# Attention: high and low parts of the probabilities joined in one product, meta keys in one product last in its unit, two output banks, dense products spread evenly over the units

## The chip, the cores and the metric

The kernel runs on one core of one Trainium2 chip. The metric is the device time of one execution in microseconds (us); of several runs the median is taken. The engines are named as in the profile: PE (TensorE, the matrix products; PEld is its loading of weights), DVE (VectorE), ACT (ScalarE), POOL (GpSimd) and SP (SyncE, which here only issues DMAs).

## The reference, cut to what matters

A block of a streaming encoder on 1024 tokens of width 1024, with 16 meta tokens ahead of them. The change lies in the attention with forgetting (8 heads of 64 channels) and in the gates that are computed beside it:

```python
h = concatenate([meta, x])                     # 16 + 1024 tokens
xn = rmsnorm(h, norm_mix_g)
q, k, v, f_logit, u, gates = split(xn @ w_in)
cum_f = cumsum(log_sigmoid(f_logit + b_forget))
s = q.k / sqrt(64) + cum_f[t] - cum_f[s]       # for s <= t, else -1e30
y_a = (softmax(s) @ v) @ w_attn_out
y_s = glu(gelu(s5(u)) @ w_glu)                 # state-space branch
g = sigmoid(gates)                             # two sets of 1024 channels
h = h + (g[:1024] * y_a + g[1024:] * y_s) @ w_o
h = h + conv_ffn(rmsnorm(h, norm_ffn_g))
out = rmsnorm(h, norm_final_g)[16:]            # meta tokens dropped
```

All is float32.

## The kernel before

**Stages.** One program goes through norm, projections, state-space branch, GLU, values, attention, output projection and ConvFFN in turn, with the next stage's loads running ahead. To keep float32 precision, each operand is split into a high part in the faster format fp32r and the rest as a low part; a dense product is three products (high by high, low by high, high by low: lines 170 to 172, `dense_steps`).

**Values.** The tile `vt` holds, for each tile of 128 keys and each head, 128 columns: 64 channels of the values' high part and 64 of the low part. The 16 meta keys are key tile 0, in rows 0 to 15.

**Attention.** The heads are taken in four pairs (loop `pr`). A pair has ten units: for each of its two heads one small unit (the 16 meta tokens as queries) and four big units of 256 queries (two tiles of 128). `scores()` makes a unit's probabilities: blocks of up to 512 columns, each in two products (lines 817 and 818, into the banks `sp`), a maximum on DVE (line 823), then the exponential on ACT and the scaling on POOL. `pv()` multiplies them by the values. The scores of a unit are issued ahead of `pv()` of the unit before, so PE has other work while the softmax runs.

**`pv()`.** The probabilities have queries in rows; for the product they are turned, so that keys lie in rows. The keys are taken in groups: the meta keys first, by themselves, then two tiles of 128 at a time, so that a big unit has one group of meta keys and one to four others. For a group, `turn()` transposes each 128x128 block on PE into the bank `tp` (line 860), ACT copies this to the high part `th` (line 867), and DVE subtracts it from the bank and writes the low part `tl` (line 868, shown as L137, the line of the helper `split_lo`). Then each key tile takes one product with `th` (line 881) and one with `tl` (line 882), both into the one output bank `po`, whose rows 0 to 63 gather what comes from the values' high part, rows 64 to 127 the rest. `turn()` of the next group is issued ahead of the products of this one. Where a key tile lies after the first query tile, half of its block is not transposed; POOL sets that half of `th` and `tl` to zero. At the end ACT copies the lower rows of `po` to `ot` (line 885) and DVE adds the halves into `ob` (line 886). The next unit's first product must wait until this has been read.

**The dense products in between.** A generator (`stream`) yields the dense products of the next pair's q and k projection and of chunks of the gates; `fill()` takes some of them at each group of a big unit. There are 28 such places a pair, and each takes what is left over the places left, rounded up. The pairs have 288, 216, 216 and 216 of these products (the first takes 24 of its own ahead). A dependency without a semaphore keeps each lot behind the fifth last group's product (`marks`, `SLACK`). Apart from it, the order in which PE takes instructions is set by the tile scheduler from the program's order and its own estimate of times. Accumulating dense products have three banks `mm`.

## Time and profile before

| | before |
|---|---|
| median of 3 runs | 1444.85 us (1443.14 to 1447.14) |
| profiled execution | 1444.9 us |
| its span | 1443.1 us |
| granted TensorE clock, mean | 0.998 |
| PE busy in the span | 1422.4 us (99%) |
| DVE, ACT, POOL busy | 1073.0, 722.2, 762.9 us |
| attention stage (first dense product after the values, to the last of its dense products) | about 340.6 to 622.3 us |

A row of PE in order of time has the start and duration in us, the engine, the line in the kernel, the operation with the tile written and the tiles read, the part of PE's array that it takes (rows*columns), its size (columns streamed after the x), and how many such instructions in a row it stands for. The duration is that from entering the array to leaving it, so that following products overlap; the distance from start to start says what one costs.

### The profile page before, as it was taken

To read this page: it belongs to the slowest core of one execution; us is meant where nothing else is said; L and a number is where in the kernel's file an instruction comes from. 1 tells how busy PE (TensorE), PEld (TensorE's weight loads), DVE (VectorE), ACT (ScalarE), POOL (GpSimd) and SP (SyncE) were. 2 spreads that over 40 slices of the span, in tenths; PEclk is the share of its full clock that TensorE was granted. 3 is DMA by queue.
4 is the path that set the end of the run, shared out by engine and by line. 5 is a ranking of instruction groups with operands and counts; after the bars stand their busy time and mean duration, and the time that the engine had idled before them with its cause. 6 is when DMAs were issued, how large, how long until landed. Compare 5 with 4: busy or idle time off the path is not lost.

```text
span 1443.1 us, 26612 instructions
## 1 busy us (share of the span) xinstructions
PE 1422.4 (99%) x9655; PEld 1346.8 (93%) x9655; DVE 1073.0 (74%) x2203; ACT 722.2 (50%) x1419; POOL 762.9 (53%) x887
## 2 busy tenths in 40 slices
PE   8999999999999999999999999999999999999997
PEld 8999999988999999999879999999999999888886
DVE  7999788843657676656469987788877876788857
ACT  7646585423656565533646544444434445644433
POOL 1542248632456556515871335555555545888794
PEclk9999999999999999999999999999999999999999
DMA  8676644530147422167964156667753327864433
GB/s 303 169 182 164 153 102 151 150 106 30 38 130 165 126 66 67 45 222 244 267 147 142 63 139 170 171 164 190 187 136 116 92 71 262 328 204 142 123 87 117
DMA packets 92968, 214.06 MB, mean 148 GB/s; under 512 B 15090, under 2 KB 22898, under 8 KB 92452
## 3 DMA queue, kind: packets, MB, share of 16 engines
q1 hardware_dynamic: 73124, 166.32, 35.2%
q0 software_dynamic: 17696, 41.29, 15.2%
q10 hardware_dynamic: 2016, 4.74, 0.9%
q8 instruction: 76, 1.25, 0.4%
q14 instruction: 56, 0.46, 0.1%
HBM read 170.88 MB, written 71.71 MB: 168 GB/s over the span
## 4 chain that ended last, share of the span: by engine, by line
PE 91%; DVE 5%; DMA 1%; ACT 1%; issue 1%; POOL 0%; SPq 0%; POOLq 0%; ACTq 0%; DVEq 0%
PE mm L172 5%; PE mm L170 5%; PE mm L171 5%; PE sp L232 4%; PE sp L233 4%; PE sp L234 4%; PE tp L232 3%; PE tp L233 3%; PE tp L234 3%; PE mm L232 3%; PE mm L234 3%; PE mm L233 3%; PE tp L860 3%; PE mm L1557 2%; PE mm L1555 2%; PE mm L1556 2%
## 5 line engine op out<-in xcount | busy, mean ns | idle before, releaser
L170 PE MATMUL mm<-xhi,whi 128*128 128x342 f32 (+2 forms) x480 | 156.8, 327 | 1.0 <-DVE q L137 1.0
L172 PE MATMUL mm<-xhi,wlo 128*128 128x342 f32 (+2 forms) x480 | 155.3, 324 | 0.0
L171 PE MATMUL mm<-xlo,whi 128*128 128x342 f32 (+2 forms) x480 | 155.2, 324 | 0.0
L1183 POOL TENSOR_TENSOR ov<-ov,og 128x1024 f32<-128x1024 f32 x21 | 50.8, 2421 | 117.1 <-ACT og L1182 114.7
L137 DVE TENSOR_TENSOR sw<-sf,sw 128x512 fp32r<-128x512 f32 x72 | 73.5, 1021 | 45.6 <-ACT sw L1174 45.3
L1174 ACT CAST sw<-sf 128x512 fp32r<-128x512 f32 x72 | 44.9, 623 | 111.3 <-POOL sf L1321 82.3
L170 PEld LDWEIGHTS mm<-xhi,whi 128*128 128x128 f32 x480 | 90.5, 188 | 2.1 <-PE sp L818 0.8
L172 PEld LDWEIGHTS mm<-xhi,wlo 128*128 128x128 f32 x480 | 90.2, 188 | 0.6 <-issue 0.2
L171 PEld LDWEIGHTS mm<-xlo,whi 128*128 128x128 f32 x480 | 90.4, 188 | 0.2
L867 ACT CAST th<-tp 128x256 fp32r<-128x256 f32 (+3 forms) x120 | 56.1, 471 | 62.5 <-PE tp L860 30.2
L137 DVE TENSOR_TENSOR tl<-tp,th 128x256 fp32r<-128x256 f32 (+3 forms) x120 | 65.2, 547 | 25.9 <-ACT th L867 24.5
L1321 POOL TENSOR_TENSOR sf<-raw,sf 128x512 f32<-128x512 f32 x36 | 63.5, 1764 | 38.7 <-DVE sw L137 38.6
L1321 POOL TENSOR_TENSOR sf<-raw 128x512 f32<-128x512 f32 x36 | 49.1, 1364 | 62.2 <-ACT sw L1174 22.2
L234 PE MATMUL mm<-xhi,sw 128*128 128x258 f32 (+1 forms) x288 | 81.0, 281 | 0.0
L232 PE MATMUL mm<-xhi,sw 128*128 128x258 f32 (+1 forms) x288 | 80.8, 281 | 0.0
L233 PE MATMUL mm<-xlo,sw 128*128 128x258 f32 (+1 forms) x288 | 80.7, 280 | 0.0
L832 POOL TENSOR_SCALAR pt<-pt,nm 128x144 f32<-128x144 f32 (+4 forms) x72 | 52.1, 736 | 49.9 <-DVE nm L831 48.9
L1373 DVE SCALAR_TENSOR_TENSOR ov<-hv,cwt,ov 128x1024 f32<-128x1024 f32 x36 | 68.5, 1904 | 0.4 <-ACT ov L1371 0.4
L1174 ACT CAST sw<-raw 128x512 fp32r<-128x512 f32 x70 | 43.0, 620 | 46.6 <-PE sp L234 22.6
L830 ACT ACTIVATE pt<-pt,nm 128x144 f32<-128x144 f32 (+4 forms) x72 | 52.9, 735 | 25.7 <-DVE nm L829 25.2
L137 DVE TENSOR_TENSOR sw<-raw,sw 128x512 fp32r<-128x512 f32 x70 | 58.3, 837 | 5.3 <-ACT sw L1174 5.1
L823 DVE CUSTOM_DVE_ANT_0 pt<-sp,fb 128x328 f32<-128x328 f32 (+8 forms) x112 | 46.4, 430 | 21.2 <-PE sp L818 12.6
(722 smaller groups left out, 5720.7 us busy)
## 6 DMA issues: line engine op xcount, KB each, us to landing
raw<-in_w_up_dram SPq DMA_DIRECT2D x44, 512.0 KB, 3.8
t_d<-in_w_dn_dram POOLq DMA_DIRECT2D x44, 256.0 KB, 6.7
wr<-t_d SPq DMA_DIRECT2D x44, 256.0 KB, 3.8
ar<-a_d SPq DMA_DIRECT2D x41, 256.0 KB, 5.2
a_d<-ov SPq DMA_DIRECT2D x18, 512.0 KB, 2.6
wr<-in_w_dn_dram SPq DMA_DIRECT2D x33, 256.0 KB, 4.0
t_d<-in_w_dn_dram SPq DMA_DIRECT2D x22, 256.0 KB, 4.7
t_d<-t_d SPq DMA_DIRECT2D x22, 256.0 KB, 4.6
```

Of the source, the lines that this page charges most:

```text
L137: return eng.tensor_tensor(out_, src, hi.bitcast(F), ALU.subtract)
L170: yield PE.matmul(ps, whi[:, i, :], ahi[:, i], start=(i == 0), stop=False)
L171: yield PE.matmul(ps, whi[:, i, :], alo[:, i], start=False, stop=False)
L172: yield PE.matmul(ps, wlo[:, i, :], ahi[:, i], start=False, stop=(i == k - 1))
L232: PE.matmul(ps, a[0][:, i], bh, start=(i == 0 and not joins), stop=False, skip_group_check=True)
L233: PE.matmul(ps, a[0][:, i], bl, start=False, stop=False, skip_group_check=True)
L234: PE.matmul(ps, a[1][:, i], bh, start=False, stop=(i == kh - 1), skip_group_check=True)
L830: S.activation(pt[:n, :kc], pt[:n, :kc], AF.Exp, bias=nm[:n, 1:2], scale=0.125, accum_out=nm[:n, 2:3])
L867: S.copy(th[:kn, z:tw], tp[:kn, z:tw])
L1174: S.copy(hi, src)
L1321: sums.append(GP.tensor_tensor(f_, a, b, op))
L1373: V.scalar_tensor_tensor(out=o, in0=h_[:, j:SEQ + j], scalar=cwc(j, m), in1=o, op0=ALU.mult, op1=ALU.add)
```

## The change

1. *Joined products.* `th` and `tl` become the two halves of one tile `tt`, and the two products of a key tile one product of 512 columns: both read the same weights, and the bank's 512 columns hold the high parts' result in the first half and the low parts' in the second. Where a key tile lies after the first query tile, only the second query tile's columns of both halves are streamed (2x128), so nothing is set to zero any more.
2. *Meta keys.* The meta values are stored twice, in rows 0 to 15 and 32 to 47 of `vt`. The meta keys' probabilities are turned into rows 0 to 15 (16 columns of weights a transpose, where 128 were taken before), the high part goes to rows 0 to 15 of a tile `tm` that is otherwise zero, the low part to rows 32 to 47, and one product of 256 columns (16 in a small unit) gives both. It is the last of its unit.
3. *Output.* The output bank is by turns `po` and one of the dense products' three `mm`. ACT copies the lower rows straight into `ob`, DVE adds the upper rows, and in a big unit the second half of the bank in a further addition.
4. *Spread.* `fill()` takes a share per unit: each big unit 1, divided evenly over its groups and one place more ahead of them; a small unit 0.4; 8.8 units a pair. In the first pair a chunk of the gates comes ahead of the q and k projection.
5. *Gates in this stage* are scaled (POOL) and stored (SP) in thirds as they come, except the last chunk.

```diff
@@ -489,14 +489,20 @@
 
     def gate_chunk(i, pl, tanh):
         whi, wlo = gate0[1:] if i == KD else wchunk(w_g[i], KD, GP, act=not tanh)
-        if tanh:
+        whole = tanh and pl is not gp_ and i == KD - 1
+        if whole:
             gs = pl.tile([P, LQ], F, tag="gs", name="gs", bufs=1)
         for t, n in QBLK[::-1] if i == KD else QBLK:
             ps = mm_ps()
             yield from dense_steps(ps[:, :n], whi, wlo, xhi[:, :, T0 + t:T0 + t + n],
                                    xlo[:, :, T0 + t:T0 + t + n], KD)
-            if tanh:
+            if whole:
                 S.activation(gs[:, t:t + n], ps[:, :n], AF.Tanh, scale=0.5)
+            elif tanh:
+                gs = pl.tile([P, LQ // 3], F, tag="gs", name="gs", bufs=2)
+                S.activation(gs, ps[:, :n], AF.Tanh, scale=0.5)
+                GP.tensor_scalar(gs, gs, 0.5, 0.5, ALU.mult, ALU.add)
+                SY.dma_start(g_d[P * i:P * i + P, t:t + n], gs)
             else:
                 if i == KD:
                     gs = g0s[:, t:t + n]
@@ -504,12 +510,9 @@
                     gs = pl.tile([P, LQ // 3], F, tag="gs", name="gs", bufs=2)
                 S.activation(gs, ps[:, :n], AF.Sigmoid)
                 GP.dma_start(g_d[P * i:P * i + P, t:t + n], gs)
-        if tanh:
+        if whole:
             GP.tensor_scalar(gs, gs, 0.5, 0.5, ALU.mult, ALU.add)
-            if pl is not gp_ and i == KD - 1:
-                okeep["g"] = gs
-            else:
-                SY.dma_start(g_d[P * i:P * i + P], gs)
+            okeep["g"] = gs
 
     def stage_gates():
         for i in range(KD, 2 * KD):
@@ -761,10 +764,15 @@
             o = ps[:n]
             if c == 0:
                 stacked(ps, vstk, wvh, wvl)
-                mv = wvp.tile([META, AW], F, name="mv")
-                S.copy(mv, ps[32:32 + n])
-                V.tensor_tensor(mv, o, mv, ALU.add)
-                o = mv
+                mv = wvp.tile([32 + META, AW], F, name="mv")
+                S.copy(mv[:n], ps[32:32 + n])
+                V.tensor_tensor(mv[:n], o, mv[:n], ALU.add)
+                V.tensor_copy(mv[32:32 + n], mv[:n])
+                p3 = mv.rearrange("p (h d) -> p h d", d=DH)
+                for r in (0, 32):
+                    S.copy(vt[r:r + n, c, :, :DH], p3[r:r + n])
+                    split_lo(V, vt[r:r + n, c, :, DH:], p3[r:r + n], vt[r:r + n, c, :, :DH])
+                continue
             else:
                 if c not in ahead:
                     lead(ps, t, n)
@@ -788,6 +796,10 @@
     qps.append(pool(st_k, "qkB", side="left"))
     ap = pool(st_a, "attn", side="left")
     KS = [META + P * c for c in range(len(TILES))]
+    tms = [ap.tile([P, n], R, name=f"tm{n}{j}") for n, j in ((256, 0), (META, 0), (META, 1))]
+    for t_ in tms:
+        GP.memset(t_.bitcast(F), 0.0)
+    n_po = [0]
     qzero = [[ap.tile([P, P], R, name=f"qz{e}{j}") for j in range(2)] for e in range(2)]
     for e in range(2):
         for z in qzero[e]:
@@ -836,19 +848,24 @@
         e = h % 2
         t, n = TILES[cs[0]]
         w = n * len(cs)
-        po = po_ps()
-        groups = [(0,)] + [(j, j + 1) for j in range(1, cs[-1], 2)]
-
+        n_po[0] += 1
+        po = po_ps() if n_po[0] % 2 else m_ps()
+        p2 = po.rearrange("p (s q) -> p s q", s=2)
+        groups = [(j, j + 1) for j in range(1, cs[-1], 2)]
+
+        def meta_keys():
+            tp = t_ps()
+            for ci, p_ in enumerate(pts):
+                PE.transpose(tp[:META, ci * n:ci * n + n], p_[:n, :META], ident[:n, :n])
+            tm = tms[0] if groups else tms[1 + e]
+            S.copy(tm[:META, :w], tp[:META, :w])
+            split_lo(V, tm[32:32 + META, :w], tp[:META, :w], tm[:META, :w])
+            return tm
         def order(grp):
             return grp[::-1] if grp[-1] > cs[0] else grp
 
-        def keys(grp):
-
-            return P if cs[0] else TILES[grp[0]][1]
-
         def turn(grp):
             tp = t_ps()
-            kn = keys(grp)
             z = 0
             for gi, kk in enumerate(order(grp)):
                 for ci, p_ in enumerate(pts):
@@ -857,46 +874,48 @@
                     if kk > cs[ci]:
                         z = o + n
                         continue
-                    PE.transpose(tp[:kn, o:o + n], p_[:n, k0:k0 + kn], ident[:n, :n])
+                    PE.transpose(tp[:, o:o + n], p_[:n, k0:k0 + P], ident[:n, :n])
             tw = len(grp) * w
-            th = ap.tile([P, 512], R, tag="th", name="th", bufs=2)
-            tl = ap.tile([P, 512], R, tag="tl", name="tl", bufs=2)
-            if z:
-                GP.memset(th[:kn, :z].bitcast(F), 0.0)
-                GP.memset(tl[:kn, :z].bitcast(F), 0.0)
-            S.copy(th[:kn, z:tw], tp[:kn, z:tw])
-            split_lo(V, tl[:kn, z:tw], tp[:kn, z:tw], th[:kn, z:tw])
-            return th, tl
-
-        nxt = turn(groups[0])
+            tt = ap.tile([P, 2, 512], R, tag="tt", name="tt", bufs=2)
+            S.copy(tt[:, 0, z:tw], tp[:, z:tw])
+            split_lo(V, tt[:, 1, z:tw], tp[:, z:tw], tt[:, 0, z:tw])
+            return tt
+
+        hooks = len(groups) + 1
+        nxt = turn(groups[0]) if groups else None
+        tm = meta_keys()
+        fill(1 / hooks if groups else SMALL)
         for g_, grp in enumerate(groups):
-            th, tl = nxt
-            kn = keys(grp)
+            tt = nxt
             if g_ + 1 < len(groups):
                 nxt = turn(groups[g_ + 1])
-            if n == P:
-                fill()
+            fill(1 / hooks)
             for gi, kk in enumerate(order(grp)):
-                last = kk == order(groups[-1])[-1]
-                PE.matmul(po[:, :w], vt[:kn, kk, h, :], th[:kn, gi * w:gi * w + w], start=(kk == 0), stop=False)
-                mk = PE.matmul(po[:, :w], vt[:kn, kk, h, :], tl[:kn, gi * w:gi * w + w], start=False, stop=last)
+                q0 = n if kk > cs[0] else 0
+                mk = PE.matmul(p2[:, :, q0:w], vt[:, kk, h, :], tt[:, :, gi * w + q0:gi * w + w],
+                               start=(g_ == gi == 0), stop=False, skip_group_check=True)
             marks.append(mk)
-        ot = ap.tile([64, 256], F, tag="ot", name="ot", bufs=1)
-        S.copy(ot[:, :w], po[64:, :w])
-        V.tensor_tensor(ob[64 * e:64 * e + 64, :w], po[:64, :w], ot[:, :w], ALU.add)
+        marks.append(PE.matmul(po[:, :w], vt[:, 0, h, :], tm[:, :w], start=not groups, stop=True,
+                               skip_group_check=True))
+        o_ = ob[64 * e:64 * e + 64, :w]
+        S.copy(o_, po[64:, :w])
+        V.tensor_tensor(o_, po[:64, :w], o_, ALU.add)
+        if groups:
+            V.tensor_tensor(o_, p2[:64, 1], o_, ALU.add)
 
     GA = [2, 1, 1, 3]
     SLACK = 5
     QKN = 2 * len(BLK) * 3 * KD
     GAN = len(QBLK) * 3 * KD
-    HOOKS = 2 * sum(1 + (c + 1) // 2 for c in range(1, len(TILES), 2))
+    SMALL = 0.4
+    UNITS = 2 * (len(TILES) // 2 + SMALL)
     stream = iter(())
     left = [0, 0]
     marks = []
 
-    def fill():
-        k = -(-left[0] // max(1, left[1]))
-        left[1] -= 1
+    def fill(share):
+        k = math.ceil(left[0] * min(1, share / max(share, left[1])))
+        left[1] -= share
         anchor = marks[-SLACK] if len(marks) >= SLACK else None
         for _ in range(k):
             if left[0] > 0:
@@ -942,8 +961,10 @@
             gens.append(gate_chunk(i, ap, True))
             cnt += GAN
         done += GA[pr]
+        if pr == 0:
+            gens[:2] = gens[1::-1]
         stream = chain_(*gens)
-        left[:] = [cnt, HOOKS]
+        left[:] = [cnt, UNITS]
         if pr == 0:
             for _ in range(24):
                 next(stream)
```

Where it moves PE's work, at three places. First, PE at the start of the second pair, where the small units stand (`sp` scores, `tp` transposed probabilities, `po` and `mm` banks of results, `tm` the meta keys' tile, `k_4187`/`q_4185` and `k_4196`/`q_4194` the same tiles of this pair). Before:

```order
L817 MATMUL sp<-k_4187,q_4185 128x400
L818 MATMUL sp<-kl,qz_4174 128x400
L817 MATMUL sp<-k_4187,q_4185 128x264
L818 MATMUL sp<-kl,qz_4173 128x264
L860 MATMUL tp<-ident,pt 128x128 x4
L881 MATMUL po<-th,vt 128x16
L882 MATMUL po<-tl,vt 128x16
L170 MATMUL mm<-xhi,whi 128x384
```

and in the changed kernel (lines 829 and 830 are what 817 and 818 were, 877 the transposes that were 860, 859 those of the meta keys, 895 the joined product, 898 the meta keys' product):

```order
L898 MATMUL mm<-tm_4176,vt 128x256
L859 MATMUL tp<-ident,pt 16x16
L898 MATMUL po<-tm_4177,vt 128x16
L829 MATMUL sp<-k_4196,q_4194 128x400
L830 MATMUL sp<-kl,qz_4183 128x400
L829 MATMUL sp<-k_4196,q_4194 128x264
L830 MATMUL sp<-kl,qz_4182 128x264
L877 MATMUL tp<-ident,pt 128x128 x3
L898 MATMUL mm<-tm_4178,vt 128x16
L859 MATMUL tp<-ident,pt 16x128 x2
L170 MATMUL mm<-xhi,whi 128x384
```

The small unit's two products have become one over all rows of the array; the transposes of the meta keys are instructions with a form of their own, and the last unit of the pair before ends with its meta keys' product.

Second, PE late in the first pair, where the scores of the last units stand (`tt` is the joined tile). Before:

```order
L172 MATMUL mm<-xhi,wlo 128x384
L817 MATMUL sp<-k_2520,q_2518 128x328
L818 MATMUL sp<-kl,qz_4176 128x328
L817 MATMUL sp<-k_2520,q_2518 128x328
L818 MATMUL sp<-kl,qz_4176 128x328
L881 MATMUL po<-th,vt 128x256
L882 MATMUL po<-tl,vt 128x256
L881 MATMUL po<-th,vt 128x256
L170 MATMUL mm<-xhi,whi 128x342
```

Changed:

```order
L877 MATMUL tp<-ident,pt 128x128 x4
L895 MATMUL po<-tt,vt 128x2x128
L895 MATMUL po<-tt,vt 128x512
L898 MATMUL po<-tm_4176,vt 128x256
L859 MATMUL tp<-ident,pt 16x128 x2
L829 MATMUL sp<-k_2520,q_2518 128x456
L830 MATMUL sp<-kl,qz_4185 128x456
L829 MATMUL sp<-k_2520,q_2518 128x456
L830 MATMUL sp<-kl,qz_4185 128x456
L877 MATMUL tp<-ident,pt 128x128 x4
L895 MATMUL mm<-tt,vt 128x512 x2
L170 MATMUL mm<-xhi,whi 128x342
```

The unit ends with its meta keys' product, its output bank changes from `po` to `mm` for the next, and the dense products stand behind the scores and the groups here.

Third, PE at the end of the first pair. Before:

```order
L860 MATMUL tp<-ident,pt 128x128 x4
L881 MATMUL po<-th,vt 128x256
L882 MATMUL po<-tl,vt 128x256
L881 MATMUL po<-th,vt 128x256
L882 MATMUL po<-tl,vt 128x256
L860 MATMUL tp<-ident,pt 128x128 x3
L881 MATMUL po<-th,vt 128x256
L170 MATMUL mm<-xhi,whi 128x272
```

Changed:

```order
L877 MATMUL tp<-ident,pt 128x128 x3
L171 MATMUL mm<-xlo,whi 128x272
L172 MATMUL mm<-xhi,wlo 128x272
L170 MATMUL mm<-xhi,whi 128x272
L171 MATMUL mm<-xlo,whi 128x272
L172 MATMUL mm<-xhi,wlo 128x272
L170 MATMUL mm<-xhi,whi 128x272
L171 MATMUL mm<-xlo,whi 128x272
L172 MATMUL mm<-xhi,wlo 128x272
L170 MATMUL mm<-xhi,whi 128x272
L171 MATMUL mm<-xlo,whi 128x272
L895 MATMUL mm<-tt,vt 128x512 x2
```

Before, the last groups of the pair stand without dense products between them; now ten stand between the last group's transposes and its products.

## The prediction

> **What bounds the kernel now.** I read the page first, then the busy time of the attention stage, then the order in time of TensorE's (PE's) instructions in it. From the page, the span and the chain of work that ended last:
>
> ```profile
> span 1443.1 us, 26612 instructions
> PE 1422.4 (99%) x9655; PEld 1346.8 (93%) x9655; DVE 1073.0 (74%) x2203; ACT 722.2 (50%) x1419; POOL 762.9 (53%) x887
> PE 91%; DVE 5%; DMA 1%; ACT 1%; issue 1%; POOL 0%; SPq 0%; POOLq 0%; ACTq 0%; DVEq 0%
> ```
>
> PE sets the end. The change lies in the attention stage, from 340.6 us (the first dense product after the values) to 622.3 us. Its busy time by engine (us, in brackets the instructions):
>
> ```profile
> core 0: us, PE busy (x) PEld busy (x) DVE busy (x) ACT busy (x) POOL busy (x), PEclk, DMA share, GB/s
> 340.60:622.30 281.70, 278.18 (x1935) 270.65 (x1934) 181.29 (x778) 160.37 (x387) 152.65 (x312) 1.00 0.33 88
> ```
>
> DVE has 100 us free in it, ACT and POOL more. So an instruction added on those three costs nothing as a sum, only where PE waits for it; the time is PE's own work, plus PE's waits. What PE's work costs is not the "mean of one" in the groups (that holds the way through the array, and overlaps) but the distance from one start to the next. PE in order of time (start, duration):
>
> ```profile
> 480.88 0.28 PE L881 MATMUL po<-th,vt 128*128 128x256 f32 x1
> 481.24 0.28 PE L882 MATMUL po<-tl,vt 128*128 128x256 f32 x1
> ...
> 337.62 0.40 PE L130 MATMUL mm<-wvl,stk 128*64 128x512 f32 x1
> 339.46 0.40 PE L130 MATMUL mm<-wvl,stk 128*64 128x512 f32 x1
> ...
> 427.09 0.60 PE L860 MATMUL tp<-ident,pt 128*128 128x128 f32 x4
> 427.62 0.27 PE L881 MATMUL po<-th,vt 16*128 16x16 f32 x1
> 427.75 0.25 PE L882 MATMUL po<-tl,vt 16*128 16x16 f32 x1
> 427.93 0.45 PE L170 MATMUL mm<-xhi,whi 128*128 128x384 f32 x1
> 428.22 0.34 PE L171 MATMUL mm<-xlo,whi 128*128 128x384 f32 x1
> 428.39 0.34 PE L172 MATMUL mm<-xhi,wlo 128*128 128x384 f32 x1
> ```
>
> Between 480.88 and 481.24 lie four products of 256 columns, three steps: 0.12 us each. Between 337.62 and 339.46 there are nine of 512 columns, eight steps: 0.23 us each. A transpose of 128 keys takes (0.60 - 0.27)/3 = 0.11 us. The last five rows are a small unit (16 queries): its two products use only 16 of the array's rows (16*128). The transposes end at 427.09 + 4 x 0.11 = 427.53, yet the second dense product starts at 428.22; of these 0.69 us one dense product of 384 columns (0.17, from 428.22 to 428.39) is useful. Leaving the full array and coming back makes two tiny products cost 0.52 us.
>
> **The change, part by part.** How many there are comes from the groups with the shapes kept apart (busy us, mean ns of one, idle before):
>
> ```profile
> L881 PE MATMUL po<-th,vt 128*128 128x256 f32 x192 | 54.6, 300 | 0.1
> L882 PE MATMUL po<-tl,vt 128*128 128x256 f32 x192 | 50.6, 286 | 1.5 <-DVE tl L137 1.4
> L137 DVE TENSOR_TENSOR tl<-tp,th 128x512 fp32r<-128x512 f32 x48 | 33.1, 690 | 14.7 <-ACT th L867 14.1 <-POOL qz L805 0.2
> L867 ACT CAST th<-tp 128x512 fp32r<-128x512 f32 x48 | 28.1, 585 | 13.6 <-PE po L881 6.0 <-PE po L882 2.8 <-PE tp L860 2.8
> L886 DVE TENSOR_TENSOR ob<-po,ot 64x256 f32<-64x256 f32 x32 | 13.3, 416 | 8.3 <-ACT ot L885 6.1 <-DMA o_d<-ob 1.4
> ```
>
> 1. *Joined products.* Of the 192 pairs of a high and a low product, 32 are the meta keys'. The other 160 become one product each. 128 of them have 512 columns: 0.23 instead of 2 x 0.12, so 128 x 0.01 = 1.3 us less. The other 32 leave out the half that was zeros (2x128 columns): 0.12 instead of 0.24, 32 x 0.12 = 3.8 us less.
>
> 2. *Meta keys in one product.* 32 pairs become one product of 256 columns: 32 x 0.12 = 3.8 us less. In the eight small units the product now has all 128 rows (zeros below), so the excursion of 0.52 us goes; 0.07 us is left for one product (its weights must be loaded; two such took 0.03 + 0.03 and 0.08 on their follower at 407.31, quoted below). 8 x 0.45 = 3.6 us less. So far 12.5 us less.
>
> 3. *The meta keys' transposes.* As many as before, 64 in the big units, but they now take 16 columns of weights (128*16, fp32) and no longer 128*128. No row of before has this transpose; the nearest is the state-space stage's product of the same form, 128*16 in fp32 with 128 columns streamed. Beside it, a pair in fp32r on 128*32:
>
> ```profile
> 91.51 0.32 PE L171 MATMUL mm<-xlo,whi 128*128 128x342 f32 x1
> 91.67 0.31 PE L172 MATMUL mm<-xhi,wlo 128*128 128x342 f32 x1
> 91.91 1.05 PE L1893 MATMUL sp<-Gm,sm 128*16 128x128 f32 x8
> 92.80 1.04 PE L1893 MATMUL tp<-Gm,sm 128*16 128x128 f32 x8
> 93.76 0.42 PE L170 MATMUL mm<-xhi,whi 128*128 128x342 f32 x1
> 94.02 0.31 PE L171 MATMUL mm<-xlo,whi 128*128 128x342 f32 x1
> ...
> 407.31 0.17 PE L817 MATMUL sp<-k,q 128*32 128x16 f32 x1
> 407.34 0.18 PE L818 MATMUL sp<-kl,qz 128*32 128x16 f32 x1
> 407.37 0.36 PE L881 MATMUL po<-th,vt 128*128 128x256 f32 x1
> 407.57 0.28 PE L882 MATMUL po<-tl,vt 128*128 128x256 f32 x1
> ```
>
> A dense product takes 0.155 (91.51 to 91.67). The one before the 128*16 row takes 0.24, 0.09 more; the sixteen take 93.76 - 91.91 = 1.85 for 16 x 0.109 = 1.75, 0.10 more; the dense one after takes 0.26, 0.10 more. So one excursion costs 0.29 us beside the 0.11 of each instruction. On 128*32 in fp32r there is almost none of it: 0.08 on the product after. The 64 new transposes stand in 42 runs of one or two in PE's changed order. Bounds: 42 x 0 and 42 x 0.30 = 12.6. I take the upper side, 42 x 0.295 = 12.4 us more, since the fp32 row has the same rows, columns and type, and the other row only the width.
>
> [...]
>
> 4. *Moved and added work on the others.* The 64 memsets on POOL go; the gates' scaling and their stores come as thirds (21 instead of 7, on POOL and SP, neither of which PE waits for in this stage). Each big unit gets one addition more on DVE: 32 x 0.416 = 13.3 us, inside the 100 us free. At nothing; if DVE were late, PE would pay up to these 13.3.
>
> 5. *Waits.* A joined product can't start on the high part alone. PE meets this already at the end of each pair of heads, where no dense product is left (the chain in order of time, then PE there):
>
> ```profile
> 552.11 0.44 PE tp L860 x4
> 552.70 0.60 ACT th L867
> 553.32 0.70 DVE tl L137
> 554.07 0.39 PE po L882
> ...
> 553.45 0.36 PE L881 MATMUL po<-th,vt 128*128 128x256 f32 x1
> 554.07 0.39 PE L882 MATMUL po<-tl,vt 128*128 128x256 f32 x1 [0.26 <-DVE tl L137]
> ...
> 617.25 0.32 PE L172 MATMUL mm<-xhi,wlo 128*128 128x342 f32 x1
> 622.32 0.32 PE L170 MATMUL mm<-xhi,whi 128*128 128x342 f32 x1
> ```
>
> From transposes to product are 0.6 (ACT) + 0.7 (DVE), with the hand-overs 1.45 us. PE covers that with the next group's transposes (0.44), the previous group's products (0.46) and dense products. At 553.45 the step is 0.62 instead of 0.12: 0.5 lost, at three pair ends 1.5 us. In the changed order ten dense products stand there (about 10 x 0.12, an estimate by columns from 0.155 for 342), so 1.5 us less. In the last unit, 617.25 to 622.32 is 5.07 us for 3.5 of work (11 x 0.11 + 18 x 0.12 + 0.155): 1.55 waiting. After, by the same legs, about 1.3 (0.5, 0.1 and 0.6 before its last three groups): 0.2 less. New is a stretch late in the first pair with six score blocks and no dense product. PE has some 6.4 us there (17 transposes, seven joined products, two meta products' worth of transposes, 2,408 score columns twice at 0.155/342 each), DVE some 7.4 (four low parts and one of 256 columns, 3.0; six blocks' maxima and two masks, 3.1; three additions, 1.3), with the maxima from this row of the page:
>
> ```profile
> L823 DVE CUSTOM_DVE_ANT_0 pt<-sp,fb 128x328 f32<-128x328 f32 (+8 forms) x112 | 46.4, 430 | 21.2 <-PE sp L818 12.6
> ```
>
> That is 1.0 us more (bounds 0 and 2.5, where DVE enters it 1.5 late).
>
> Sum: -12.5 + 12.4 - 1.5 - 0.2 + 1.0 = -0.8 us. The profiled execution took 1444.9 us (1.8 around its span), the median of the runs shown is 1444.85: **1444.1 us, no change**. A difference under 0.3% (4.3 us) can't be told from none.
>
> **The rivals.**
>
> *A. The 16-column transposes cost no excursion.* For it: the pair at 407.31, and that the row at 91.91 is no transpose. Against: type and form are the latter's, and the small units' excursion shows that PE pays for leaving the full array. Then 12.4 us fall away: 1431.7 us. If half of it shows (runs hidden in waits, or cheaper beside other transposes), 1438 us.
>
> *B. The low part becomes the wait.* The dense products are now shared evenly over units, so a unit with four groups has 24.5 of them over five places (216 over 8.8 units' worth in three of the four pairs), 4.9 x 0.155 = 0.76 us a group, where it had 216/28 = 7.7, 1.2 us. Cover per group is 0.44 + 0.46 + 0.76 = 1.66 against 1.45: 0.2 us to spare. DVE also does two maxima of 0.43 per group in these units, each of which can stand ahead of the low part. A group without cover loses 0.5 (553.45). The units of three and four groups have 14 groups a pair, 56 in all; a third of them uncovered is 19 x 0.5 = 9.5 us: 1453 us. It decides from about ten groups on. Against: DVE is busy 181 of 282 us, and PE's order puts dense products behind most transposes.
>
> *C. The spread removes all waits, or none.* Within 3 us of the sum, so part of the forecast.
>
> **How the numbers follow.** The forecast 0.54 (its own range 1440 to 1449), A 0.24, half of A 0.08, B 0.14. Faster by over 0.3% (below 1440.5): A nearly whole 0.23, half of A 0.05, the forecast's lower tail 0.07: 0.35. Slower (above 1449.2): B 0.13 and the upper tail 0.06: 0.19. Within: 0.46. The range of 8 in 10 reaches from A's middle, 1432 (0.12 left below), nearly to B's middle, 1452 (0.08 above).
>
> **What would show it.** In the profile after: two 256-column products turned into one with a step of 0.23, and 0.12 for 2x128. The dense or score product before a 128*16 transpose with a step 0.09 longer, the one after 0.10; if the steps stay at 0.155 and 0.12, A holds. No 16*128 rows. At the three pair ends no wait of a `po` product for a low part; if PE's joined products show waits for DVE in the middle of pairs, B holds. The busy time of DVE in the stage rises by some 13 us without moving PE. The forecast is wrong if the steps around the 128*16 transposes are plain, or if more than ten joined products wait.

## The result, and the profile after

The changed kernel takes 1462.56 us (median of 4 runs, 1459.21 to 1464.66), the kernel before 1445.08 us; the ratio is 1.0119 (95% interval 1.0103 to 1.0135). It is 17.5 us slower, and outside the predicted range of 1432 to 1452. Two executions of the experiments below, one of e5 (6452 us) and one of e8 (3591 us), are in the slow state and left out of every median. The page of the changed kernel, against the lines shown of before:

```profile
span 1461.5 us, 26185 instructions
PE 1424.4 (97%) x9455; PEld 1334.6 (91%) x9455; DVE 1087.8 (74%) x2237; ACT 721.2 (49%) x1420; POOL 758.5 (52%) x840
PE 93%; DVE 3%; ACT 1%; issue 1%; DMA 1%; POOL 0%; POOLq 0%; SPq 0%; ACTq 0%; DVEq 0%
```

PE has 200 instructions less and is busy 2 us longer. The time went in the attention stage alone (the rest is 2.3 us shorter). Below is its busy time, from the first dense product after the values to the first product of the next stage, with 1008 dense products in it in both kernels; the stretch of the table ahead, to 622.3 us, ends 72 dense products earlier (length, then busy and instructions of PE, PEld, DVE, ACT, POOL, then the granted clock). Before:

```profile
340.40:633.60 293.20, 289.68 (x2008) 282.12 (x2007) 184.42 (x782) 164.16 (x393) 152.65 (x312) 1.00 0.35 97
```

After:

```profile
339.50:653.40 313.90, 292.08 (x1809) 270.05 (x1808) 199.69 (x816) 163.17 (x395) 146.09 (x264) 0.97 0.31 91
```

The stage is 20.7 us longer. PE is idle for 21.8 us of it (313.90 - 292.08) where it was 3.5, and the granted clock is 0.97 where it was 1.00, which is some 10 us more (worked out below). DVE has 15 us more to do, where 13 were forecast, and is still free for 114 us. What PE waited for, in us, with the number of waits and the longest; before, from 340 to 640 us:

```profile
PE po L882 <- DVE tl L137: 1.4, 5, 0.3
PE mm L170 <- DVE q L137: 1.0, 2, 0.5
PE sp L817 <- DVE mx L823: 0.6, 1, 0.6
```

and after, from 345 to 660 us:

```profile
PE sp L829 <- DVE mx L835: 8.7, 12, 1.8
PE tp L877 <- DVE tt L137: 4.5, 4, 1.5
PE tp L877 <- DVE nm L841: 2.3, 2, 1.8
PE mm L898 <- DVE tm L137: 2.0, 2, 1.0
PE mm L895 <- DVE tt L137: 1.5, 2, 0.8
PE sp L829 <- DVE ob L902: 1.2, 1, 1.2
PE sp L830 <- POOL qz L817: 0.5, 1, 0.5
...
```

All of them but one are waits for DVE, and the largest is one that was hardly there: a score block waits until DVE has taken the maximum out of its bank. How it looks in PE's order of time, late in the third pair:

```profile
528.53 0.40 PE L895 MATMUL po<-tt,vt 128*128 128x512 f32 x1
528.76 0.28 PE L898 MATMUL po<-tm,vt 128*128 128x256 f32 x1
528.88 0.27 PE L859 MATMUL tp<-ident,pt 128*16 128x128 f32 x1
528.99 0.49 PE L877 MATMUL tp<-ident,pt 128*128 128x128 f32 x3
...
529.34 0.43 PE L829 MATMUL sp<-k,q 128*128 128x392 f32 x1
529.61 0.34 PE L830 MATMUL sp<-kl,qz 128*128 128x392 f32 x1
529.78 0.31 PE L829 MATMUL sp<-k,q 128*128 128x328 f32 x1
529.93 0.31 PE L830 MATMUL sp<-kl,qz 128*128 128x328 f32 x1
530.78 0.39 PE L829 MATMUL sp<-k,q 128*128 128x328 f32 x1 [0.54 <-DVE mx L835]
531.01 0.31 PE L830 MATMUL sp<-kl,qz 128*128 128x328 f32 x1
532.84 0.55 PE L877 MATMUL tp<-ident,pt 128*128 128x128 f32 x3 [1.51 <-DVE tt L137]
533.14 0.97 PE L895 MATMUL mm<-tt,vt 128*128 128x512 f32 x2
533.91 0.52 PE L170 MATMUL mm<-xhi,whi 128*128 128x384 f32 x1
```

The single steps are as forecast or better (512 columns 0.23, meta keys 0.12, a 16-column transpose 0.11). But the score blocks stand one behind the other with no dense product between them, so that each wait is open; and the last two rows have become slow: a dense product of 384 columns lasts 0.52 us, where one at full clock lasted 0.34 (428.22, before).

Why DVE is late though it is not full shows in its queue at the same kind of place in the first pair (DVE in order of time):

```profile
395.21 0.15 DVE L841 TENSOR_SCALAR nm<-nm 128x1 f32<-128x1 f32 x1
396.54 0.16 DVE L843 RECIPROCAL nm<-nm 128x1 f32<-128x1 f32 x1 [1.17 <-ACT pt L842]
396.62 0.61 DVE L835 CUSTOM_DVE_ANT_0 pt<-sp,fb 128x456 f32<-128x456 f32 x1
...
398.36 1.12 DVE L137 TENSOR_TENSOR kl<-mm,k 64x384 fp32r<-64x384 f32 x2 [0.49 <-ACT k L613]
399.51 0.53 DVE L835 CUSTOM_DVE_ANT_0 pt<-sp,fb 128x352 f32<-128x352 f32 x1
```

with PE beside it:

```profile
397.29 0.43 PE L829 MATMUL sp<-k,q 128*128 128x352 f32 x1 [1.09 <-DVE mx L835]
...
400.10 0.51 PE L829 MATMUL sp<-k,q 128*128 128x336 f32 x1 [1.53 <-DVE mx L835]
```

DVE takes its instructions in order, as these rows show: the reciprocal of the unit before waits 1.17 us for ACT's exponential, and the maximum that would free the bank stands behind it, though PE had finished its scores by 394.97; the next maximum stands behind two low parts of the next pair's keys (1.12 us), which had waited 0.49 us for ACT as well. So PE waits less for the maxima's own work than for what stands ahead of them in DVE's queue, while nothing stands on PE to fill the time.

After this stretch the clock is halved. PE's busy time and clock in steps of 4 us (length, busy, instructions, clock):

```profile
396.00:400.00 4.00, 1.35 (x6) 1.00 0.18 37
400.00:404.00 4.00, 3.90 (x14) 0.57 0.48 185
...
532.00:536.00 4.00, 3.17 (x12) 0.68 0.00 0
```

Summed over the stage by such steps it is 10 us. In finer steps the clock stands at 0.50 from about 400.3 to 403.7 us, 3.4 us that cost 1.7; there are four such stretches, from 400.29, 434.42, 461.73 and 533.40 us, and a double one from 352.50. In order of time these starts lie 47.79, 34.13, 27.31 and 71.67 us apart: 14, 10, 8 and 21 times 3.41. In the 3.41 us ahead of the four PE was busy for 1.34, 2.31, 1.36 and 1.36 us, ahead of the double one for 1.94. In two other stretches of 3.41 us, from 345.68 and from 625.56 us, which lie such multiples away as well, it was busy for 2.09 and 2.01, and no half clock followed. So PE's busy time alone doesn't part the two cases here.

### The profile page after: what moved, and what is told of

It reads as the page before. It is cut to its first block, busy times and chain, and to the rows that moved or that the text cites. A ratio compares the mean times of both kernels' runs of the same rounds, so it can differ in the third digit from the quotient of the medians.

```text
span 1461.5 us, 26185 instructions
## 1 busy us (share of the span) xinstructions
PE 1424.4 (97%) x9455; PEld 1334.6 (91%) x9455; DVE 1087.8 (74%) x2237; ACT 721.2 (49%) x1420; POOL 758.5 (52%) x840
## 4 chain that ended last, share of the span: by engine, by line
PE 93%; DVE 3%; ACT 1%; issue 1%; DMA 1%; POOL 0%; POOLq 0%; SPq 0%; ACTq 0%; DVEq 0%
PE mm L170 5%; PE mm L172 5%; PE mm L171 5%; PE sp L233 4%; PE sp L232 4%; PE sp L234 4%; PE mm L232 3%; PE mm L234 3%; PE tp L232 3%; PE tp L233 3%; PE mm L233 3%; PE tp L234 3%; PE tp L877 2%; PE mm L1578 2%; PE mm L1576 2%; PE mm L1577 2%
## 5 line engine op out<-in xcount | busy, mean ns | idle before, releaser
L137 DVE TENSOR_TENSOR tt<-tp,tt 128x512 fp32r<-128x512 f32 (+1 forms) x80 | 50.3, 633 | 21.6 <-ACT tt L880 21.2
L880 ACT CAST tt<-tp 128x512 fp32r<-128x512 f32 (+1 forms) x80 | 42.9, 539 | 37.2 <-PE tp L877 36.7
```

The source lines that it names most:

```text
L137: return eng.tensor_tensor(out_, src, hi.bitcast(F), ALU.subtract)
```

## The experiments

All times are medians; the kernel before stood at 1443.6 to 1445.0 us beside them. "Stage" is the time of the stage above in the profiled run (before 293.2, changed 313.9).

**First: is it the spread, DVE's added work, or the 16-column transposes?**

e1, on the changed kernel:

```diff
-        fill(1 / hooks if groups else SMALL)
+        if groups: fill(1)
-            fill(1 / hooks)
+            fill(1)
-    UNITS = 2 * (len(TILES) // 2 + SMALL)
+    UNITS = 28            # places of a pair, as before
```

> The changed kernel with the earlier sharing of the dense products alone put back (one share at each group of a big unit, none in small units, 28 places a pair). Theory 1 (the even spread takes the dense products away from the score blocks of the long units, PE then waits there for DVE's maxima, and the clock halves after it): the 21 us of waits fall to about 7, the 10 us at half clock go, and the time is about 1462.6 - 14 - 10 = 1438 us (1433 to 1444). Theory 2 (the waits come from the joined product, which needs the low part, from the second addition and the shared banks): at least 1455 us, with the waits for maxima and low parts as they are.

Measured: 1467.59 us (1.0148, 1.0118 to 1.0179); stage 315.1. The earlier spread doesn't mend it, so theory 1 falls. Its waits for maxima are 9.1 us, as in the changed kernel.

e2, on the kernel before: `fill(share)`, `UNITS` and `SMALL` of the changed kernel, each big unit's share divided over its groups.

> The kernel before with the even sharing alone (each big unit 1, over its groups; a small unit 0.4; 8.8 a pair), products, transposes and banks as they were. Theory 1: PE waits for maxima in the long units as in the changed kernel, and the clock halves some times: 1445 + 12 to 25 = 1457 to 1470 us. Theory 2: within 4 us of 1445.

Measured: 1452.77 us (1.0052, 1.0034 to 1.0070); stage 299.9, clock 1.00. Between the two: the even spread does cost 8 us alone, without half clock, and isn't the main cause. Of the stage's 6.7 us only 2.7 are idle time of PE; for the other 4 it counts as busy with the same products. So the waits may cost more than their idle time: in the changed kernel a row behind one lasts longer (328 columns 0.39 us at 530.78, and 0.31 at 531.01).

e3, on the changed kernel:

```diff
-        if groups:
-            V.tensor_tensor(o_, p2[:64, 1], o_, ALU.add)
```

> The changed kernel without the further addition of the bank's second half in the big units, so that what the low parts of the probabilities give is left out of the output: 32 x 0.42 = 13.3 us less on DVE and nothing else. Theory 1: within 4 us of the changed kernel's 1462.6. Theory 2 (DVE too late by its added work): 1455 us or less.

Measured: 1455.44 us (1.0071, 1.0052 to 1.0089); stage 306.9. The 13.3 us of additions on DVE are worth 7 us, at an engine that is free for 114. Theory 1 falls with it, and theory 2 is missed by only 0.4 us; but 10 us of the loss stay, so this is a part and not the whole.

e4, on the changed kernel:

```diff
-  PE.transpose(tp[:META, ...], p_[:n, :META], ident[:n, :n])
+  PE.transpose(tp[:P, ...], p_[:n, :P], ident[:n, :n])     # big units
```

> The changed kernel with the meta keys' transposes over 128 columns of weights, of which 16 rows are read (128*128, as the other transposes) in the big units. If the 16-column form cost 0.29 us a run as the prediction had it, 42 x 0.29 = 12 us less: about 1450 us. If it costs nothing, as the steps beside it in the changed kernel's trace say (0.268 us for transpose and dense product together, against 0.266 without a change of form): within 4 us of 1462.6.

Measured: 1463.87 us (1.0133, 1.0112 to 1.0154), as the changed kernel, with PE's instructions in the same order. The 16-column form costs nothing; PE in the changed kernel around one of them:

```profile
485.71 0.28 PE L898 MATMUL mm<-tm,vt 128*128 128x256 f32 x1
485.83 0.27 PE L859 MATMUL tp<-ident,pt 128*16 128x128 f32 x1
485.85 0.40 PE L172 MATMUL mm<-xhi,wlo 128*128 128x342 f32 x1
486.10 0.32 PE L170 MATMUL mm<-xhi,whi 128*128 128x342 f32 x1
```

From 485.71 to 485.83 is the plain step of 256 columns, and from 485.83 to 486.10 there are 0.27 us for a transpose and a dense product: 0.11 + 0.155, with nothing on top.

**Second: the output bank.**

e5, on the changed kernel, and e6, on the kernel before, the same line both ways:

```diff
-        po = po_ps() if n_po[0] % 2 else m_ps()
+        po = po_ps()                                # e5
```

> The changed kernel with one output bank: every unit's output goes to the bank po, as before, and the dense products keep their three banks. Theory 3 (an output that takes one of the dense products' three banks by turns makes the scheduler put the dense products in clumps of 15 to 24, so that score blocks stand six and eight in a row without them, and PE waits there for DVE's maxima and then runs at half clock): in this kernel's order at most two score blocks stand in a row, the 21 us of waits fall to about 7, no stretch at half clock is left, and the time is 1436 to 1446 us. Theory 2 (the joined product's need of the low part, and DVE's further additions): at least 1453 us.

> The kernel before with the two output banks alone (by turns po and one of the dense products' three). Theory 3: score blocks stack up (up to four in a row in the order), waits for maxima of 10 us or more and stretches at half clock: 1452 us or more. Theory 2: within 4 us of 1445, or faster, since a second output bank lets the next unit's products start earlier.

Measured: e6 1469.35 us (1.0175, 1.0158 to 1.0192), stage 320.8: the second output bank alone costs 25 us on a kernel that has all its old products. Its waits begin with

```profile
PE sp L818 <- DVE mx L824: 8.6, 8, 2.0
PE po L883 <- DVE nm L832: 4.1, 1, 4.1
```

and its clock in the stage is 0.97. But e5 is 1457.02 us (1.0095, 1.0074 to 1.0116), stage 306.6, only 5.5 us better than the changed kernel, and in the range of theory 2. The waits for maxima go, as theory 3 said, and another takes their place:

```profile
PE tp L877 <- DVE tt L137: 9.6, 5, 3.5
PE tp L877 <- DVE nm L841: 2.8, 2, 1.5
PE sp L829 <- DVE mx L835: 1.7, 4, 0.6
```

A transpose waits for its bank until DVE has made the low part out of it. The two longest of these waits, 3.46 us each, are 6.9 of the 9.6 us; one of them, with ACT and DVE ahead of it:

```profile
446.17 0.47 ACT L608 CAST k<-mm 64x384 fp32r<-64x384 f32 x1 [3.39 <-PE mm L172]
448.13 1.12 DVE L137 TENSOR_TENSOR kl<-mm,k 64x384 fp32r<-64x384 f32 x2 [4.45 <-ACT k L613]
449.29 0.69 DVE L137 TENSOR_TENSOR tt<-tp,tt 128x512 fp32r<-128x512 f32 x1
450.03 0.90 PE L877 MATMUL tp<-ident,pt 128*128 128x128 f32 x3 [3.46 <-DVE tt L137]
```

ACT stood idle for 3.39 us ahead of the copies of the next pair's keys, until PE had finished their dense products; DVE stood idle behind it for 4.45, and the low part behind the keys'. So this, too, is a queue in order, and not the group without cover that the prediction's second rival priced; that 9.6 us is near its 9.5 is chance.

e8 puts both back, one bank and the earlier spread; what is left are the joined products, the meta keys last and the gates in thirds. e7 has the joined products alone on the kernel before:

```diff
-  PE.matmul(po[:, :w], vt[:kn, kk, h, :], th[...], ...)
-  PE.matmul(po[:, :w], vt[:kn, kk, h, :], tl[...], ...)
+  PE.matmul(p2[:, :, q0:w], vt[:kn, kk, h, :], tt[:kn, :, ...], ...)
+  V.tensor_tensor(o_, p2[:64, 1], o_, ALU.add)    # at the unit's end
```

> The changed kernel with one output bank and the earlier sharing of the dense products: what is left of the change is the joined products, the meta keys in one product last in the unit, and the gates in thirds. Theory 3: products 12 us less than before and waits about as before: 1432 to 1442 us; and the even spread by itself is worth at most some 8 us against it (e2 showed 1452.8 for it alone). Theory 2: at least 1450 us.

> The kernel before with the joined products alone (the big units' meta keys as a group of their own, joined as well; small units as before; one output bank; the further addition on DVE; the earlier spread). Products: 128 x 0.005 + 32 x 0.118 + 32 x 0.005 = 4.6 us less. Theory 3: waits as in the kernel before, or 3 us more; 1438 to 1445 us. Theory 2: PE waits for the low parts, 1452 us or more.

Measured: e8 1445.41 us (1.0013, 1.0004 to 1.0023), stage 297.5; e7 1447.81 us (1.0030, 1.0019 to 1.0041), stage 298.3; both lie between the two expectations. So putting back the second bank and the spread together takes away all but 2 of the 17 us lost; one alone put back gives -5.5 or +5. And neither kernel gains what its products save: e7 is 5 us longer in the stage, with 4.6 less in products.

**Third: what of the bank, what of the meta keys, and does saved work count?**

e12 holds a bank without using it for outputs, on the kernel before:

```diff
+  hb = None if n_po[0] % 2 else m_ps()
+  # at the unit's first and last group: a product of 16 columns into hb;
+  # at its end ACT copies 16 columns of hb (not used)
```

> The kernel before, every output in po, but in every second unit one of the dense products' three banks is held from the unit's first group to its last (two added products of 16 columns, their result read by ACT and not used): 40 products and 20 copies, some 2 to 5 us by themselves (16 of these columns' products in small units use 16 rows). Theory 3a (the dense products' lack of a bank makes the lots and the waits): 1455 us or more, waits for maxima and stretches at half clock as with two output banks (1469). Theory 3b (the second bank for outputs moves the products of the next unit ahead, and that makes the waits): 1444 to 1450 us.

Measured: 1470.13 us (1.0172, 1.0158 to 1.0186), stage 321.6, as long as with two output banks. Of the 28 us more, some 8 are the added products' own: 36 x 0.12 us of work (a small unit has one of them, not two), and 3.5 us in which they wait for a high part. The rest, some 20 us, goes with the bank that the dense products lack. In PE's order the dense products then stand in lots (with no other product between them; the stage's first and last lot left out) of up to 25 (before, up to 16), and up to six score blocks stand between two lots (before, four at one place and elsewhere two); with two output banks it is 21 and eight, in the changed kernel 24 and six.

PE's waits for maxima go roughly with these score blocks. They are at most 1.8 us in the kernels with three in a row, or four at one place only; 3.5 to 5.2 in e8, e10 and e3, with four to six; and 7.6 to 9.1 in e12, e6, e1 and the changed kernel, with six to eight. They go less with the lots: e8 has 20 of 16 products or more, the changed kernel 16.

e10 has the meta keys' part alone on the kernel before; e14 moves a unit's first place for dense products to its end; e15 leaves out the zero half as well:

```diff
-        if groups: fill()            # e10: ahead of the first group
         for g_, grp in enumerate(groups):
             ...
+        if groups: fill()            # e14: behind the last one
         marks.append(PE.matmul(po[:, :w], vt[:, 0, h, :], tm[:, :w], ...))
```

> The kernel before with the meta keys' part alone: transposed to 16 columns, high and low in one product, last in the unit, all 128 rows in the small units, the output copied straight into ob; the other products apart as before, one output bank, the earlier shares. Products 3.8 us less, excursions 3.6 less, the transposes' form 0. Without new waits: 1443.6 - 7.4 = 1436 us. Theory 3 in the wider form (whatever makes the dense products stand in lots of 16 instead of 8 gives part of it back, and so they stand here, since the first two places of a unit are no longer parted by the meta keys' products): 1438 to 1446 us.

> The kernel of e10 (meta keys in one product, last in the unit, on the kernel before; 1459.6 us) with the first of a unit's places for dense products moved behind its last group, ahead of the meta keys' product, so that a group's products stand between any two places. Theory 3 in the wider form (two places with nothing between them make lots of 16 dense products, and score blocks without any): at most two score blocks stand between dense products in this order, and the time is 1436 to 1445 us. Rival (the meta keys' product last in the unit is late by itself, waits on ACT and DVE, and delays the output): 1452 us or more.

> e14 with the zero half left out as well: by e9 another 1.6 to 3.8 us less than e14. Theory 3: 1433 to 1442 us.

Measured: e10 1459.63 us (1.0098, 1.0084 to 1.0112), 15 us slower with less work on PE, outside of both expectations. e14 1449.16 us (1.0036, 1.0022 to 1.0049): moving one call gives 10 of the 15 back, which speaks for the lots (19 lots of 16 or more in e10, 10 in e14, 9 before). The other 5 us stay, between the two expectations, though e14's lots are those of before: its products wait 4.7 us for low parts (1.4 before) and 1.7 for high parts. So the place of the meta keys' product has a part that the lots don't explain. e15 1446.11 us (1.0019, 1.0010 to 1.0029), above what was expected.

e9 and e13 are small edits: the zero half left out with products apart (e9), and the small units' two products over all 128 rows besides (e13). They were meant to leave PE's order alone, but the scheduler moved it: neither has a lot of 16 dense products or more, where the kernel before has 9. e11 has the meta keys in one product, but first in the unit, and the zero half left out:

```diff
+  q0 = n if kk > cs[0] else 0
-  PE.matmul(po[:, :w], vt[:kn, kk, h, :], th[:kn, gi * w:gi * w + w], ...)
+  PE.matmul(po[:, q0:w], vt[:kn, kk, h, :], th[:kn, gi * w + q0:gi * w + w], ...)   # and tl
```

> The kernel before with the zero half left out alone: where a key tile lies after the first query tile, its two products stream the second query tile's 128 columns and nothing is set to zero; no joined tile, no further addition. 64 products of 256 columns become 64 of 128: 64 x 0.059 = 3.8 us less, the order as regular as before. Theory 3: 1443.6 - 3.8 = 1440 us (1437 to 1442). If products don't set the time here (theory 4: PE's work in this stage is worth nothing because waits take up what is saved): within 1.5 us of 1443.6.

> The kernel before with the zero half left out, and the small units' two products over all 128 rows (tiles zeroed once); the output copied straight into ob; all else as before, no wait added and the order as regular as before. Products 3.8 us less, and 8 x (0.52 - 0.07) = 3.6 us less for the excursions to 16 rows. Theory 3 (order decides, and saved work counts where the order stays): 1442.7 (e9) - 3.6 = 1439 us (1437 to 1441). Theory 4 (saved work turns into waits): 1442 us or more.

> The kernel before with the savings that add nothing on DVE: meta keys transposed to 16 columns and in one product, but first in the unit as before; zero half left out; products of high and low apart; one output bank; the earlier shares. Products 3.8 + 3.8 and excursions 3.6 us less; the dense products stand in lots of 14 at most, at most three score blocks between them. Theory 3: 1443.6 - 11.2 = 1432.4 us (1430 to 1436). Theory 4: 1440 us or more.

Measured: e9 1442.67 us (0.9990, 0.9981 to 0.9998), stage 292.7; e13 1443.72 (0.9997, 0.9988 to 1.0005), stage 292.7; e11 1444.63 (0.9996, 0.9985 to 1.0006), stage 294.0. Of the 3.8, 7.4 and 11.2 us expected, 1.6, 0 and 0 arrived, and of e9's 1.6 only 0.5 stand in the stage. Most of e9's was never there. PE in e9, where a dense product, a half product and two whole ones follow on each other:

```profile
382.65 0.32 PE L172 MATMUL mm<-xhi,wlo 128*128 128x342 f32 x1
382.81 0.23 PE L881 MATMUL po<-tl,vt 128*128 128x128 f32 x1
382.87 0.33 PE L879 MATMUL po<-th,vt 128*128 128x256 f32 x1
383.04 0.28 PE L881 MATMUL po<-tl,vt 128*128 128x256 f32 x1
```

The half product takes 0.06 (382.81 to 382.87), but the one behind it 0.17 instead of 0.12: 0.11 in all against 0.12, so that 64 of them save some 0.6 us and not 3.8. (The joined form, one instruction of 2x128 columns, does keep its 0.12.) In e13 two products of 16 columns over all rows:

```profile
562.40 0.71 PE L863 MATMUL tp<-ident,pt 128*128 128x128 f32 x5
562.86 0.26 PE L882 MATMUL po<-zt,vt 128*128 128x16 f32 x1
562.97 0.26 PE L884 MATMUL po<-zt,vt 128*128 128x16 f32 x1
563.09 0.40 PE L172 MATMUL mm<-xhi,wlo 128*128 128x342 f32 x1
563.33 0.32 PE L170 MATMUL mm<-xhi,whi 128*128 128x342 f32 x1
```

From the transposes' end (562.40 + 5 x 0.11 = 562.95) to 563.33 are 0.38 us for a dense product of 0.155 and 0.22 besides, where the two over 16 rows cost 0.52: 0.3 a unit, 2.4 us, not 3.6. These didn't arrive: e13's stage is no shorter than e9's. PE is busy for 1.8 us less in it (287.3 against 289.1) and idle for 1.9 more, with nearly the same order. Of e11's work some 7 us were real by these steps (3.8 the meta keys in one product, 2.6 the small units, 0.6 the half), and its stage is 0.8 us longer, with 5.6 us more idle time, 2.8 of it waits for the meta keys' low part, and a clock of 0.99. Theory 4 holds in part: the smaller saving goes into waits. e9 is the only kernel with the whole computation that is clear of the one before on the fast side, by 0.1%; whether its products or its order did that isn't shown.

e16 is e7 without the addition:

> The kernel of e7 (joined products alone on the kernel before, 1447.8 us) without the further addition of the bank's second half, so that what the low parts of the probabilities give is left out of the output. If the 9 us that e7 waits more than before come from the addition on DVE and what it holds up: 1439 to 1441 us (products 4.6 us less). If they come from the joined product's need of the low part: 1445 to 1448 us.

Measured: 1442.52 us (0.9994, 0.9985 to 1.0003), stage 291.6, between the two expectations. Leaving out the addition gives back 5 us of the 9 or so that e7 waits (5 us longer in the stage with 4.6 us less work). It also moved PE's order (e7 has 11 lots of 16 or more, e16 none), so that the 5 us are the addition's together with that order's. Without it the stage is 1.6 us shorter than before where 4.6 were saved, so that the need of the low part and the rest take 3 us at most.

## Why the prediction was wrong, point by point

- **The bound and the products** (parts 1 and 2): nearly right (8.2 us in the big units, where 8.9 were forecast). The steps are 0.23 for 512 columns and 0.12 for 256 (rows from 528.53). By these steps the big units' products took 384 x 0.118 = 45.3 us before and 128 x 0.23 + 64 x 0.12 = 37.1 after. Only the small units were overrated: their one product costs about 0.2 (0.11, and 0.08 on the product behind it, as in e13) and not 0.07, so that 2.6 us go there and not 3.6. PE's work fell by some 11 us.
- **The meta keys' transposes** (part 3): wrong by its whole 12.4 us. e4 and the rows at 485.83 show nothing. No row of before has a transpose of this form, and of the two nearest rows I took the wrong one. Rival A was right here, and one of the forecast's own signs of being wrong came: plain steps around these transposes. Products over 16 rows did pay (0.52 us a pair in the kernel before), transposes to 16 columns didn't. With this term right, the sum would have been 1432 us and farther from what was measured.
- **Work on the other engines at nothing** (part 4): failed. "Inside the 100 us free" was true and worth nothing. The addition costs 7 us in the changed kernel (e3) and 5 in e7 (e16, with the order that went with it); DVE works in order (rows from 395.21), and what stands in its queue holds a bank (PE waits 3.46 us for one in e5, at 450.03). The sentence "if DVE were late, PE would pay up to these 13.3" was the right bound; I took its lower end.
- **The output bank**: named in the account of the change and not priced in the prediction. Alone it costs 25 us (e6), and a bank held without any output in it some 20 (e12). It should have been a term, with its bounds: a unit takes some 7 us (40 in 293), and the bank held for that time is one of three.
- **Waits** (part 5): this is the step that failed, with part 4 and the bank inside it. I forecast 1.7 us less around the pair ends and in the last unit and 1.0 more in one stretch, 0.7 less in all. Measured are 18 us more idle time and some 10 us at half clock. Apart from that stretch I priced the waits of joined products for the low part, and those are small: three, 1.8 us, none at the pair ends. PE waits for DVE instead ahead of score blocks (9.9 us) and transposes (6.8 us), which need a free bank and no low part. The stretch with six score blocks that I priced at 1.0 us (bounds 0 and 2.5) waits 1.09 + 1.53 us and then runs 3.4 us at half clock. I summed what DVE has to do there and compared sums; the queue's order (the reciprocal, the low parts of the next keys) wasn't in it.
- **The clock**: not in the prediction at all; some 10 us of the changed kernel's stage. In its trace the clock stands at 0.50 for 3.41 us four times and for 6.83 once. The longest wait there is 1.8 us, and PE was busy for 1.34 to 2.31 of the 3.41 us ahead of the drops, while 2.09 and 2.01 us brought none (345.68, 625.56). What brings a drop isn't shown beyond these readings.
- **Rival B** had the right sign, at a price of 9.5 us and a chance of 0.14. Its mechanism isn't what happened: it had joined products wait in groups without cover, from about ten on, and three wait. Low parts do come late, but for transposes that need the bank (4.5 us in the changed kernel, 9.6 in e5), and it had neither the score blocks nor the clock.

The stage in terms: 18 us more idle, about 10 at half clock, some 11 us of work less: 17 of the 20.7 us. The rows that last longer behind a wait (0.39 us for 0.31, at 530.78) are part of the other 4; how much isn't worked out. The parts don't add up either: alone on the kernel before they cost 8, 25, 4 and 15 us, together 18. All of them reorder PE's instructions, and no run but e4 keeps the order of the kernel that it edits. What is shown is what each edit costs with the order that comes of it; why the scheduler stacks score blocks when a bank is held is argued from the order, not shown.

## What to carry to other kernels

Work taken off an engine that is 99% busy counted here only in part or not at all, even where its order hardly moved (e13 against e9); first look for what an edit does to banks, places and queues, and price those. An engine's free time says nothing of whether its next instruction comes in time: look at what stands ahead of it in the queue. In the changed kernel, waits of up to 1.8 us on TensorE cost 1.7 us more each time 3.41 us at half clock followed. That filler belongs where the waits are, and not spread evenly, is argued; no run here places it so.

## What the runs showed of the hardware

- Transposes in fp32 to 16 columns of weights (128*16) cost no more than those to 128 (0.11 us, nothing on their neighbours: rows from 485.83, and e4), while products over 16 rows (16*128) cost 0.52 us a pair (before, from 427.62). The sixteen products on 128*16 at 91.91 paid 0.29 us; why these transposes pay nothing isn't shown.
- A product of 16 columns over all rows has a step of 0.11 us to the next like it (e13, 562.86 to 562.97), and one of 128 columns takes 0.06 and delays the next by 0.05 (e9, from 382.81). These are products in fp32r, as are those of 256 columns at 0.12 us (before, from 480.88); in fp32 a product of 130 columns took 0.11 (before, L1973 from 112.31 to 112.53, two).
- In the changed kernel's attention stage the clock stands at 0.50 for 3.41 us four times and for 6.83 us once. PE was busy for 1.34 to 2.31 us of the 3.41 ahead of these stretches, and for 2.09 and 2.01 us of two that no half clock followed. The kernel before has no half clock in this stage (its mean there 1.00).
